# Scaling the tokens by their RMS factors before a plain transposition, in place of a product with a scaled identity

## The chip, the cores and the metric

The kernel runs on one core of a Trainium2 chip. The metric is the device time of one execution in microseconds (us), the median of several executions. A core has TensorE (PE in the profile, PEld its weight loads), VectorE (DVE), ScalarE (ACT), GpSimd (POOL) and SyncE (SP), each with a queue of instructions that it runs in order.

## The reference

Two layers of a diffusion backbone work on 512 latent tokens and 256 context tokens of width 1024. What matters here is the frame around the big products:

```python
def rms_norm(x, g):
    y = x * lax.rsqrt(jnp.mean(x * x, axis=-1, keepdims=True) + EPS)
    return y * g

for i in range(DEPTH):                      # DEPTH = 2
    h = modulate(rms_norm(x, norm_mix_pre[i]), sh1, sc1)
    m = mixing_sublayer(h, ...)             # ends with ... @ w_out[i], the out projection
    x = x + g1 * rms_norm(m, norm_mix_post[i])
    f = swiglu(modulate(rms_norm(x, norm_ffn_pre[i]), sh2, sc2), ...)
    x = x + g2 * rms_norm(f, norm_ffn_post[i])
```

In the second layer only the latent tokens go on to the output. All is in float32.

## The kernel before, in words

Tokens lie in six tiles of 128: tiles 0 and 1 are context, 2 to 5 latent. The second layer's out projection and FFN treat tiles 2 to 5 alone. The big products run on TensorE as three passes each (`mm3`, lines 142 to 144), because weights and activations are split in a high and a low part; `wblock` loads a block of weights (line 136, SP queue), ScalarE writes the high part (line 131) and VectorE the low one (line 132). Activations enter those products transposed, with the 1024 channels on the partitions: `hhi` and `hlo`.

At the end of an out projection (`out_proj`, lines 1089 to 1104) and of the first layer's FFN (`ffn`, lines 1190 to 1219) each token tile takes these steps:

1. ScalarE squares and sums the product (`square`, line 1026), VectorE multiplies it by the gate.
2. `residual`: GpSimd turns the sums into the factor of the post norm (`rsq`, lines 185, 187 and 188), VectorE adds the scaled product to the old tokens `xt` (line 1031).
3. GpSimd's queue issues the DMA of the new tokens to DRAM (line 1099 or 1212).
4. `norm_tile`: ScalarE sums the squares of the new tokens (line 330, two instructions), GpSimd makes the factor of the pre norm (lines 187 and 188), and ScalarE scales the 128x128 identity by it (line 337). The scaled identity `dg` lies in the first 128 columns of the tile's row in `ut` (out projection) or `mt` (FFN), where it shows in the profile as u or m.
5. After every second tile, `to_hT` transposes and scales the pair at once: for each of eight blocks of 128 channels, and for each of the two tiles, a matmul of 128x128 with the tokens as stationary operand and `dg` as moving one (line 147). Four of these fill one PSUM bank; the banks are the single ones of the pools pr and md in turn. ScalarE applies the modulation (line 351, two instructions for each bank), VectorE splits the result (lines 355 and 356).

There are 16 such tiles, in eight pairs: three pairs at the first out projection (profile 346 to 384 us), three at the end of the first FFN (946 to 986 us), two at the second out projection (1149 to 1183 us). The text calls these places site 1, 2 and 3. The same `to_hT` also serves the very start of the kernel with another call of `norm_tile`.

The order of instructions on each engine is set when the program is built: a planner simulates the engines with its own costs and gives each engine the next instruction that it holds to be ready, earlier lines of the program first. On the chip each engine then follows its list, whatever comes late.

Of the kernel before, what the change touches and what calls it, by code (L numbers as in the profile page):

```python
# [14 lines left out]
AF = mybir.ActivationFunctionType  # L15
ALU = mybir.AluOpType
# [68 lines left out]
def tile_backbone(ctx, tc, A, out):  # L85
# [60 lines left out]
    def mm(ps, lhsT, rhs, start=True, stop=True, **k):  # L146
        return PE.matmul(ps, lhsT, rhs, start=start, stop=stop, skip_group_check=True, **k)  # L147
# [185 lines left out]
    def norm_tile(x, dg, junk):  # L333

        ss = sumsq(x, junk)
        r = rsq(ss, 1, 1.0 / D)
        S.activation(dg, ident, AF.Copy, scale=r[:, 0:1])

    def to_hT(l, sub, pr, xs, dg, hhi, hlo, k2s=range(4), start=False):
        lane = 1 if pr == 0 else 0  # L340
        for k2 in k2s:
            ps = acc() if start else (mdt if k2 % 2 else prt)()
            for kk in range(2):
                for i in range(2):
                    k = 2 * k2 + kk
                    mm(ps[:, 256 * kk + 128 * i:256 * kk + 128 * i + 128],
                       xs[i][:, 128 * k:128 * k + 128], dg[i])
            h32 = sp.tile([128, 2, 256], F32, tag="h32", name=nm("h32"), bufs=2)
            for kk in range(2):
                k = 2 * k2 + kk  # L350
                last_s[0] = S.activation(h32[:, kk], ps[:, 256 * kk:256 * kk + 256], AF.Identity,
                                         scale=cols[l][:, 2 * sub, lane, k:k + 1],
                                         bias=cols[l][:, 2 * sub + 1, lane, k:k + 1])
            o = (slice(None), slice(2 * k2, 2 * k2 + 2), slice(256 * pr, 256 * pr + 256))
            V.tensor_copy(hhi[o], h32)
            last_v[0] = V.tensor_sub(hlo[o], h32, hhi[o])  # L356
# [680 lines left out]
    def out_proj(l, mac, Gs):  # L1037

        lat_only = l == DEPTH - 1
        tiles = list(range(2, 6)) if lat_only else list(range(6))  # L1040
        w_out = A["w_out"][l].rearrange("(k p) c -> p k c", p=128)
        src = [(mac, 0), (mac, 1), None, None, None, None, (mac, 2), (mac, 3)]
        order = (0, 6, 2, 4)

        def run(rnd, h, pss, ks=order):
            def one(i, k, w):
                o = slice(128 * i, 128 * i + 128)
                t_, c_ = src[k]
                mm3(pss[i], t_[:, 0, c_, o], t_[:, 1, c_, o], w[0][:, k % 2], w[1][:, k % 2],
                    k == order[0], k == order[-1] + 1)  # L1050

            last = {}
            for n, k in enumerate(ks):
                w = wblock(w_out[:, k:k + 2, 512 * h:512 * h + 512], [128, 2, 512])
                if ks[-1] == order[-1] and n >= len(ks) - 2 and h == 1:
                    last[k] = last[k + 1] = w
                    continue
                for kk in range(2):
                    for i in rnd:
                        one(i, k + kk, w)  # L1060
            for i in rnd:
                for k, w in last.items():
                    one(i, k, w)

        pss0 = {i: acc() for i in tiles[:3]}
        if lat_only:
            pss0[tiles[3]] = mdt()
        run(list(pss0), 0, pss0, order[:2])
        mb = yield
        for n in range(4):  # L1070
            src[2 + n] = (mb, n)
        late = [i for i in tiles if i not in pss0]
        for i in late:
            pss0[i] = aux()
        if late:
            run(late, 0, pss0, order[:2])
        h2 = [bigt([128, 8, 768], F32R, "h2") for _ in range(2)]
        ut = bigt([128, 6, 1024], F32, "u")
        sq = sums()
        half = 2 if lat_only else 3  # L1080
        xts, dg = {}, {}
        Gs = Gs()
        for rnd, h in ((tiles, 0), (tiles[:half], 1), (tiles[half:], 1)):
            pss = pss0 if h == 0 else {i: (acc if i in tiles[:min(half, 3)] else aux)() for i in rnd}
            if h == 1:
                for i in rnd:
                    xts[i] = q4([128, 1024], s="xt")
                    dma(xts[i], xd[i])
            run(rnd, h, pss, order if h else order[2:])
            for i in rnd:  # L1090
                square(pss[i], sq[i], h)
                c_ = slice(512 * h, 512 * h + 512)
                V.tensor_mul(ut[:, i, c_], pss[i], Gs[1 if i < 2 else 0][:, c_])
                if h == 0:
                    continue
                xt = xts[i]
                residual(xt, ut[:, i], sq[i])
                xo = dr.tile([128, 1024], F32, name=nm("xd"))
                dmap(xo, xt)
                xd[i] = xo  # L1100
                dg[i] = ut[:, i, 0:128]
                norm_tile(xt, dg[i], ut[:, i])
                if i % 2 == 1:
                    to_hT(l, 1, i // 2, (xts[i - 1], xts[i]), (dg[i - 1], dg[i]), *h2)
        yield h2

    def ffn(l, h2, filler):
# [5 lines left out]
        wg = A["ffn_w_gate"][l].rearrange("(k p) c -> p k c", p=128)  # L1113
        wu = A["ffn_w_up"][l].rearrange("(k p) c -> p k c", p=128)
        wd = A["ffn_w_down"][l].rearrange("(f p) c -> p f c", p=128)
        xts, dg = {}, {}
        act = [bigt([128, 8, 768], F32R, "act") for _ in range(2)]
        mt = bigt([128, 6, 1024], F32, "m")
        for pi, (f0, nf) in enumerate(parts):
# [61 lines left out]
            for rnd, h in rounds:  # L1181
# [11 lines left out]
                for i in rnd:  # L1193
# [6 lines left out]
                    if last and h == 1:  # L1200
                        xt = xts[i]
                        if lat_only:
                            r = rsq(sq[i][:, 0:1], 1, 1.0 / D, more=sq[i][:, 1:2])
                            for hf in range(2):
                                c_ = slice(512 * hf, 512 * hf + 512)
                                V.scalar_tensor_tensor(xt[:, c_], mt[:, i, c_], r[:, 0:1], xt[:, c_],
                                                       op0=ALU.mult, op1=ALU.add)
                                dma(out[0, 128 * (i - 2):128 * (i - 2) + 128, c_], xt[:, c_])
                            continue
                        residual(xt, mt[:, i], sq[i])  # L1210
                        xo = dr.tile([128, 1024], F32, name=nm("xd"))
                        dmap(xo, xt)
                        xd[i] = xo
                        dg[i] = mt[:, i, 0:128]
                        norm_tile(xt, dg[i], mt[:, i])
                        if i == 1:
                            hnext.extend(bigt([128, 8, 768], F32R, "h") for _ in range(2))
                        if i % 2 == 1:
                            to_hT(l + 1, 0, i // 2, (xts[i - 1], xts[i]), (dg[i - 1], dg[i]), *hnext)

    hnext = []

# [144 lines left out]
```

## Time and profile before

| what | value |
|---|---|
| median of three runs | 1559.03 us |
| the three runs | 1552.45, 1559.03, 2079.58 us |
| the profiled execution | 1553.79 us |
| its span, first to last instruction | 1552.0 us |
| mean granted TensorE clock in it | 0.987 of full |
| busy share of TensorE, VectorE, ScalarE, GpSimd | 95%, 54%, 41%, 10% |
| DMA, mean over the span | 162 GB/s |

The third run is a disturbed one. The profile lists for every instruction its start and its length. A matmul's length includes its way through the array, so a row of x8 matmuls that lasts 1.05 us with matmuls of 0.27 us each starts one every (1.05 - 0.27) / 7 = 0.11 us. The idle time in brackets behind a row is that of the engine just before it, with what ended it.

### The profile page before, as it was taken

What the parts mean: (1) busy time and instruction counts of PE and PEld (TensorE: products, weight loads), DVE (VectorE), ACT (ScalarE), POOL (GpSimd) and SP (SyncE); (2) the same over time, 40 slices, a digit from 0 to 9 for tenths busy, and PEclk for the clock granted to TensorE, in tenths of its full rate; (3) what the DMA queues carried; (4) which work ended last, traced back from release to release, by engine and by line L of the source; (5) the groups of instructions that cost most, each with busy time, mean ns of one, the idle gap of its engine ahead of it and who ended that gap; (6) DMA issues with size and microseconds to landing.
All of it is one profiled execution on the core that took longest, in us unless ns stands there. A gap on an engine that the chain in (4) does not pass through costs nothing.

```text
span 1552.0 us, 22603 instructions
## 1 busy us (share of the span) xinstructions
PE 1475.9 (95%) x8777; PEld 1227.6 (79%) x8777; DVE 841.0 (54%) x1479; ACT 630.7 (41%) x1182; POOL 161.1 (10%) x281
## 2 busy tenths in 40 slices
PE   4899898999999999999999999999988999999996
PEld 3766695888888778888778887899778888888885
DVE  5977864646465676445763336587555332333334
ACT  3778564446323234233222215656454223222222
POOL 1113210012000010000010005211011000000003
PEclk9999999999999999999999999999999999999998
DMA  9788987773334455333674314768474333333332
GB/s 294 246 274 262 306 273 220 254 181 108 92 109 121 138 185 175 111 95 118 209 261 128 95 62 130 235 170 240 112 265 135 95 95 97 99 102 97 96 95 82
DMA packets 219487, 250.68 MB, mean 162 GB/s; under 512 B 41806, under 2 KB 164058, under 8 KB 218868
## 3 DMA queue, kind: packets, MB, share of 16 engines
q1 hardware_dynamic: 209268, 214.26, 45.5%
q0 software_dynamic: 9344, 34.58, 6.4%
q8 instruction: 69, 1.13, 0.3%
q10 hardware_dynamic: 768, 0.40, 0.1%
q14 instruction: 38, 0.31, 0.1%
HBM read 206.76 MB, written 42.43 MB: 161 GB/s over the span
## 4 chain that ended last, share of the span: by engine, by line
PE 81%; DMA 9%; DVE 4%; ACT 3%; POOL 1%; issue 1%; SPq 1%; DVEq 0%; POOLq 0%; ACTq 0%
PE acc L142 20%; PE acc L144 19%; PE acc L143 19%; PE aux L144 4%; PE aux L142 4%; PE aux L143 4%; PE pr L147 3%; PE md L147 3%; PE aux L147 2%; DMA F<-Fd 2%; DMA raw<-in_w_out_dram 1%; DMA wm<-in_w_mod_dram 1%; DVE w L132 1%; DMA raw<-in_w_in_dram 1%; PE acc L147 1%
## 5 line engine op out<-in xcount | busy, mean ns | idle before, releaser
L142 PE MATMUL acc<-h,w 128*128 128x512 f32 (+1 forms) x1248 | 430.1, 346 | 1.2 <-ACT w L131 0.8
L144 PE MATMUL acc<-h,w 128*128 128x512 f32 (+1 forms) x1248 | 428.4, 344 | 2.8 <-DVE w L132 2.8
L143 PE MATMUL acc<-h,w 128*128 128x512 f32 (+1 forms) x1248 | 429.5, 345 | 1.5 <-DVE h L356 1.4
L132 DVE TENSOR_TENSOR w<-raw,w 128x1024 fp32r<-128x1024 f32 x190 | 233.0, 1227 | 335.1 <-ACT w L131 332.3
L131 ACT CAST w<-raw 128x1024 fp32r<-128x1024 f32 x190 | 199.3, 1050 | 411.7 <-PE acc L143 231.3
L142 PEld LDWEIGHTS acc<-h,w 128*128 128x128 f32 x1248 | 235.8, 190 | 33.6 <-issue 3.4
L144 PEld LDWEIGHTS acc<-h,w 128*128 128x128 f32 x1248 | 236.1, 189 | 33.1 <-DVE w L132 3.6
L143 PEld LDWEIGHTS acc<-h,w 128*128 128x128 f32 x1248 | 236.3, 189 | 30.8 <-DVE h L356 2.3
L1142 DVE TENSOR_TENSOR fsg<-fsg,acc 128x512 f32<-128x512 f32 (+1 forms) x68 | 39.8, 585 | 159.7 <-PE acc L144 156.8
L144 PE MATMUL aux<-w,act 128*128 128x512 f32 x220 | 86.2, 393 | 0.0
L143 PE MATMUL aux<-w,act 128*128 128x512 f32 x220 | 86.2, 392 | 0.0
L144 PE MATMUL acc<-w,act 128*128 128x512 f32 x220 | 86.0, 391 | 0.0
L143 PE MATMUL acc<-w,act 128*128 128x512 f32 x220 | 85.8, 390 | 0.0
L142 PE MATMUL aux<-w,act 128*128 128x512 f32 x220 | 82.7, 390 | 0.0
L142 PE MATMUL acc<-w,act 128*128 128x512 f32 x220 | 82.5, 392 | 0.0
L266 DVE SCALAR_TENSOR_TENSOR macc<-wm,csil,macc 128x1024 f32<-128x1024 f32 x56 | 70.6, 1278 | 5.5 <-DMA wm<-in_w_mod_dram 5.4
L1143 ACT CAST act<-fsg 128x512 fp32r<-128x512 f32 (+1 forms) x68 | 36.5, 537 | 87.5 <-DVE fsg L1142 87.5
L1141 ACT ACTIVATE fsg<-acc 128x512 f32<-128x512 f32 (+1 forms) x68 | 34.8, 511 | 81.4 <-PE acc L144 81.4
L143 PE MATMUL acc<-w,h 128*128 128x512 f32 (+1 forms) x160 | 55.6, 348 | 1.1 <-DVE w L132 1.1
L147 PE MATMUL md<-wm,csil 128*32 128x256 f32 (+1 forms) x416 | 35.6, 404 | 21.1 <-DMA wm<-in_w_mod_dram 21.1
L144 PE MATMUL acc<-w,h 128*128 128x512 f32 (+1 forms) x160 | 55.2, 345 | 0.0
L142 PE MATMUL acc<-w,h 128*128 128x512 f32 (+1 forms) x160 | 53.9, 354 | 0.0
(370 smaller groups left out, 2322.8 us busy)
## 6 DMA issues: line engine op xcount, KB each, us to landing
wm<-in_w_mod_dram SPq DMA_DIRECT2D x90, 512.0 KB, 4.3
raw<-in_ffn_w_gate_dram SPq DMA_DIRECT2D x44, 512.0 KB, 3.9
raw<-in_ffn_w_up_dram SPq DMA_DIRECT2D x44, 512.0 KB, 3.8
raw<-in_ffn_w_down_dram SPq DMA_DIRECT2D x44, 512.0 KB, 3.8
raw<-in_w_in_dram SPq DMA_DIRECT2D x28, 512.0 KB, 5.0
raw<-in_w_out_dram SPq DMA_DIRECT2D x26, 512.0 KB, 6.9
xt<-xd SPq DMA_DIRECT2D x18, 512.0 KB, 4.9
Ed<-Et POOLq DMA_DIRECT2D x16, 512.0 KB, 4.7
```

Source lines behind the costliest of these rows:

```text
L131: S.copy(hi, raw)
L132: last_v[0] = V.tensor_sub(lo, raw, hi)
L142: PE.matmul(ps, lhi, rhi, start=start, stop=False, skip_group_check=True)
L143: PE.matmul(ps, lhi, rlo, start=False, stop=False, skip_group_check=True)
L144: return PE.matmul(ps, llo, rhi, start=False, stop=stop, skip_group_check=True)
L147: return PE.matmul(ps, lhsT, rhs, start=start, stop=stop, skip_group_check=True, **k)
L266: V.scalar_tensor_tensor(accs[r], raw, c_, accs[r], op0=ALU.mult, op1=ALU.add)
L1141: S.activation(sg[:, :n], p1[:, :n], AF.Silu)
L1142: V.tensor_mul(sg[:, :n], sg[:, :n], p2[:, :n])
L1143: S.copy(act[0][:, fl, o:o + n], sg[:, :n])
```

## The change

A new helper writes the scaled tokens themselves: ScalarE the first 512 channels, GpSimd the other 512, both into the tile's row of `ut` or `mt`. `to_hT` then gets these rows and no `dg`, and transposes them with the unscaled identity. The start of the kernel keeps the old way.

```diff
+    def norm_scaled(x, dst):
+
+        r = rsq(sumsq(x, dst), 1, 1.0 / D)
+        S.activation(dst[:, 0:512], x[:, 0:512], AF.Copy, scale=r[:, 0:1])
+        GP.tensor_scalar(dst[:, 512:1024], x[:, 512:1024], r[:, 0:1], None, op0=ALU.mult)
+
     def to_hT(l, sub, pr, xs, dg, hhi, hlo, k2s=range(4), start=False):
...
-                    mm(ps[:, 256 * kk + 128 * i:256 * kk + 128 * i + 128],
-                       xs[i][:, 128 * k:128 * k + 128], dg[i])
+                    o = ps[:, 256 * kk + 128 * i:256 * kk + 128 * i + 128]
+                    x_ = xs[i][:, 128 * k:128 * k + 128]
+                    PE.transpose(o, x_, ident) if dg is None else mm(o, x_, dg[i])
...
-                dg[i] = ut[:, i, 0:128]
-                norm_tile(xt, dg[i], ut[:, i])
+                norm_scaled(xt, ut[:, i])
                 if i % 2 == 1:
-                    to_hT(l, 1, i // 2, (xts[i - 1], xts[i]), (dg[i - 1], dg[i]), *h2)
+                    to_hT(l, 1, i // 2, (ut[:, i - 1], ut[:, i]), None, *h2)
...
-                        dg[i] = mt[:, i, 0:128]
-                        norm_tile(xt, dg[i], mt[:, i])
+                        norm_scaled(xt, mt[:, i])
...
-                            to_hT(l + 1, 0, i // 2, (xts[i - 1], xts[i]), (dg[i - 1], dg[i]), *hnext)
+                            to_hT(l + 1, 0, i // 2, (mt[:, i - 1], mt[:, i]), None, *hnext)
```

## Rows read from the trace of the kernel before

**Rows 1.** The page, part 1: busy us, share of the span, instructions of each engine.

```profile
PE 1475.9 (95%) x8777; PEld 1227.6 (79%) x8777; DVE 841.0 (54%) x1479; ACT 630.7 (41%) x1182; POOL 161.1 (10%) x281
```

**Rows 2.** Groups of TensorE by line and shape: busy us, mean ns | idle before.

```profile
L147 PE MATMUL pr<-u,xt 128*128 128x128 f32 x80 | 13.7, 310 | 5.2 <-ACT u L337 3.9 <-ACT h L351 1.3
...
L147 PE MATMUL md<-u,xt 128*128 128x128 f32 x80 | 12.4, 292 | 1.5 <-ACT h L351 1.5
...
L147 PE MATMUL pr<-m,xt 128*128 128x128 f32 x48 | 7.1, 280 | 1.1 <-ACT h L351 1.1
L147 PE MATMUL md<-m,xt 128*128 128x128 f32 x48 | 7.0, 279 | 0.4 <-ACT h L351 0.4
...
L533 PE MATMUL pr<-ident,Cr 128*128 128x128 f32 x16 | 2.9, 313 | 0.0
```

**Rows 3.** Timeline of TensorE at and behind site 1: start us, us, instruction, count.

```profile
357.16 1.05 PE L147 MATMUL pr<-u,xt 128*128 128x128 f32 x8
...
363.28 1.65 PE L147 MATMUL pr<-u,xt 128*128 128x128 f32 x6 [0.83 <-ACT u L337]
...
378.04 0.83 PE L147 MATMUL pr<-u,xt 128*128 128x128 f32 x6
...
412.73 0.60 PE L533 MATMUL pr<-ident,Cr 128*128 128x128 f32 x4
```

**Rows 4.** Timeline of ScalarE at site 1.

```profile
364.97 1.02 ACT L351 ACTIVATE h<-pr,cols 128x256 f32<-128x256 f32 x2 [1.74 <-PE pr L147]
...
374.33 0.40 ACT L337 ACTIVATE u<-ident,rs 128x128 f32<-128x128 f32 x1 [0.96 <-POOL rs L188]
```

**Rows 5.** Stretches: length, busy of PE, PEld, DVE, ACT, POOL, clock, DMA.

```profile
360.00:365.00 5.00, 2.69 (x12) 2.31 (x13) 4.21 (x6) 2.35 (x6) 2.44 (x5) 0.79 0.62 210
370.00:380.00 10.00, 10.00 (x54) 8.58 (x53) 2.80 (x5) 5.00 (x10) 2.23 (x4) 1.00 0.13 52
946.00:961.00 15.00, 15.00 (x70) 12.49 (x69) 10.82 (x15) 8.19 (x18) 6.77 (x16) 1.00 0.19 74
961.00:980.00 19.00, 15.62 (x116) 13.79 (x115) 15.14 (x23) 15.04 (x33) 10.71 (x21) 1.00 0.89 286
```

**Rows 6.** Two lines of GpSimd: ns of one, shortest/median/longest, first and last start.

```profile
L798 POOL COPY wk<-PT x16: 498/1027/5005, 77.6 to 1067.6; 128x384 f32<-128x384 f32 x16
...
L1198 POOL TENSOR_TENSOR m<-m,G x10: 1282/1300/2272, 936.2 to 1527.8; 128x512 f32<-128x512 f32 x10
```

**Rows 7.** Groups of ScalarE by line and shape: busy us, mean ns.

```profile
L1143 ACT CAST act<-fsg 128x512 fp32r<-128x512 f32 x42 | 26.1, 621 | 84.4 <-DVE fsg L1142 84.4
...
L337 ACT ACTIVATE u<-ident,rs 128x128 f32<-128x128 f32 x10 | 4.0, 402 | 8.1 <-POOL rs L188 8.1
```

**Rows 8.** Timeline of GpSimd at site 2, tile 3 to tile 4.

```profile
967.28 0.33 POOL L187 TENSOR_SCALAR rs<-ss 128x1 f32<-128x1 f32 x1 [0.68 <-ACT m L330]
...
968.83 0.39 POOL L187 TENSOR_SCALAR rs<-rs 128x1 f32<-128x1 f32 x1
969.30 0.55 POOL L188 TENSOR_TENSOR rs<-rs,mhalf 128x1 f32<-128x1 f32 x1
```

**Rows 9.** Timeline of VectorE at site 2.

```profile
938.51 1.79 DVE L132 TENSOR_TENSOR w<-raw,w 128x1024 fp32r<-128x1024 f32 x1
...
969.88 1.28 DVE L1031 SCALAR_TENSOR_TENSOR xt<-m,rs,xt 128x1024 f32<-128x1024 f32 x1 [0.72 <-POOL rs L188]
```

**Rows 10.** Timelines of ScalarE and TensorE at the last tile of site 2.

```profile
979.05 0.40 ACT L337 ACTIVATE m<-ident,rs 128x128 f32<-128x128 f32 x1 [0.19 <-POOL rs L188]
...
979.50 0.94 PE L147 MATMUL pr<-m,xt 128*128 128x128 f32 x6
```

**Rows 11.** Timelines of GpSimd and TensorE at site 3.

```profile
1169.22 1.78 POOL L187 TENSOR_SCALAR rs<-ss 128x1 f32<-128x1 f32 x1 [0.36 <-ACT u L330]
...
1169.13 0.39 PE L144 MATMUL acc<-h,w 128*128 128x256 f32 x1 [1.79 <-DVE w L132]
...
1177.24 0.94 PE L147 MATMUL pr<-u,xt 128*128 128x128 f32 x6 [2.11 <-ACT u L337]
```

More of the change, by code (lines that the diff above doesn't have):

```diff
@@ L1080, in out_proj @@
         half = 2 if lat_only else 3
-        xts, dg = {}, {}
+        xts = {}
         Gs = Gs()
@@ L1115, in ffn @@
         wd = A["ffn_w_down"][l].rearrange("(f p) c -> p f c", p=128)
-        xts, dg = {}, {}
+        xts = {}
         act = [bigt([128, 8, 768], F32R, "act") for _ in range(2)]
```

## Prediction, made before the changed kernel was built

> **What bounds the kernel now.** I read the page's busy shares first: TensorE is busy for 95% of the span [rows 1], so time goes where its work goes, except where it waits. Next came the groups of TensorE, to see what the edited matmuls cost and what they wait for. They show 80 + 80 + 48 + 48 = 256 instructions for 16 tiles of 8 channel blocks, so each float32 matmul is two passes; and their waits are 5.2 + 1.5 + 1.1 + 0.4 = 8.2 us, half of that on the scaled identity [rows 2]. Then the timelines and stretches of the three sites, to see whether TensorE or the chain from tile to tile sets the pace. At site 1 TensorE waits for the second pair (2.69 us busy of 5 at a mean granted clock of 0.79) and is full through the third (10.00 of 10) [rows 5]. At site 2 it is full up to 961 us and busy for 15.62 of the next 19 us, while VectorE and ScalarE are busy for 15 each [rows 5]. There the pace is that of a chain: VectorE's residual is released by GpSimd 0.72 us after it was free [rows 9], and GpSimd had made that factor directly behind the factor of the tile before [rows 8]. The last tile's matmuls start 0.05 us after its identity is ready [rows 10]. At site 3 the last pair is waited for, 2.11 us [rows 11].
>
> **TensorE's part.** Eight half passes last 1.05 us: one starts every 0.11 us [rows 3]. Plain transpositions of the same shape are in the trace: line 533 transposes 2 x 2 x 4 = 16 blocks, and has 16 instructions [rows 2], four of them in 0.60 us, again 0.11 us apart [rows 3]. So a transposition costs half of a scaling matmul. A pair goes from 32 instructions to 16 and saves 16 x 0.111 = 1.78 us of TensorE; eight pairs save 14.2 us. That is the most that the edit can give.
>
> **ScalarE's part.** 16 scalings of the identity, 0.40 us each, give way to 16 of 128x512. The same engine's cast of 128x512 is 0.62 us [rows 7]; I take 0.60, so +0.2 us in each tile's chain. The squares, the sums and the factor stay.
>
> **GpSimd's part.** 16 new instructions on 128x512, price p. Below: a copy of 128x384 took 0.50 us at its shortest [rows 6], by columns 0.50 x 512 / 384 = 0.67 us, and a little less if a part of it is fixed. Above: the product of two 128x512 tiles, 1.28 us alone and 2.27 at its longest [rows 6]. Nearest is the copy, one input as here; I take p = 0.65 and keep 0.5 to 2.27 for the range. The Trainium skill (GPSIMD Engine Reference, 3.1, Elementwise) gives a measured 769 ns for 512 elements in a tight one-input loop; with that figure the sum below would be 0.7 us higher.
>
> TensorE needs this half only from the third bank of a pair on, and the banks pr and md come free at ScalarE's pace (1.02 us for each bank, [rows 4]); so for the pair itself p is hidden up to about 2 us (0.6 for ScalarE's half, 0.4 for the first bank's four transpositions, 1.0 until that bank is free). What is queued behind it on GpSimd matters more. The planner takes earlier lines of the program first, so the new instruction should stand behind the factor of tile i and ahead of the last step of the factor for tile i+1, for which VectorE's residual waits. Where one tile's factor directly follows another's, as in [rows 8], each handover costs p. There are four at site 1, five at site 2, two at site 3. GpSimd's queue also issues the DMA of the new tokens, now p later; they are read back behind it on the SP queue, but the next weights on that queue are more than 10 us away, so I cost that at nothing. If that cover were gone, it would be p once per tile. Tokens come free earlier, since TensorE no longer reads them: nothing, as no wait names them.
>
> **The sum by sites.**
> - Site 1: of the first pair's halves one (0.9 us) is among products without waits; the other ends in a wait for ScalarE and counts nothing. The second pair is exposed: ScalarE waited 1.74 us for its first bank [rows 4], behind six half passes at the low clock (1.65 us, [rows 3], against 0.83 for the same six at full clock); three transpositions would come 0.7 us sooner, less 0.2 for ScalarE: -0.5. The third pair: -1.78, TensorE being full there [rows 5]; its last tile's identity is ready at 374.7 us [rows 4] and used at 378.0 [rows 3], so the two handovers ahead of it are covered by 3.3 us. Sum -3.2 us.
> - Site 2: the first two pairs' relief (3.6 us) is lost in the wait for tile 5, for [rows 10] show no slack. Handovers 5 x p, less about 0.5 us of slack at the early tiles, where TensorE is full [rows 5]; +0.2 for ScalarE. The last pair -1.6. Sum 5p - 1.9 = +1.35 us.
> - Site 3: the first pair's relief falls in a wait for weights (1.79 us on line 132, [rows 11]): nothing, and its handover likewise. Handover from tile 4 to 5: p + 0.2. The last pair ran at a lowered clock; paced by ScalarE, I take -1.0. Sum p - 0.8 = -0.15 us.
>
> Together 6p - 5.9 = -2.0 us at p = 0.65. Against the profiled execution's 1553.79 us (span 1552.0 and 1.8 around it) this gives **1552 us**. The median shown is 5.2 us above that execution, with only three runs, one disturbed; a new median may stand as far off, which the range takes in.
>
> **Rivals.**
> - **GpSimd becomes the slower link** (slower than before). p decides at 1.0 us: above it 6p - 5.9 is a loss. For it: VectorE and GpSimd hold each other up here. A factor step of 128x1, 0.19 us elsewhere, took 1.78 us while VectorE split tokens [rows 11], the product of line 1198 went from 1.28 to 2.27 [rows 6], and VectorE's split beside it took 1.79 [rows 9]. At p = 2.27 the sum is +7.7, and two handovers (4.5 us) outrun the 3.3 us of slack at site 1, +1.2: 1553.8 + 8.9 = 1562.7 us. Against it: the planner may put the scaling where GpSimd waits for the residual, 1.3 us each time. The Trainium skill (SBUF — State Buffer, Who interferes with whom) says that a VectorE instruction with two SBUF inputs and a GpSimd instruction that reads SBUF exclude each other for the whole instruction, whoever comes first. The rows named here agree with it; by that rule taken alone every handover would cost the long price. Chance 0.2.
> - **TensorE's relief counts in full**: the planner fills the gaps with other products, and the scaling stands off the chain. 1553.8 - 14.2 = 1539.6 us. For it: the 95% of [rows 1]. Against it: the waits at all three sites [rows 2]. Chance 0.15.
> - **The planner's list changes far from the sites**, with weights and products in another order; either sign, of unknown size, and the one way to more than 2%. Chance 0.06.
> - **A plain transposition is no cheaper** (two passes after all): nothing gained, 6p + 0.6 lost, 1558 us. [Rows 2] speak against it, 16 calls and 16 instructions. Chance 0.02.
>
> **Numbers.** The forecast, 1545 to 1558 us by its own bounds (p from 0.5 to 1.3, a pair more or less), has 0.57. The range 1540 to 1564 reaches to the full relief and to the long price. 2% is 31 us, about what a measurement of this kernel can tell from no change; no case worked out comes near it, only a re-planned program could: faster 0.02, same 0.95, slower 0.03.
>
> **What the changed profile would show.** 128 transpositions at sites 1 to 3 in place of 256 half passes, 0.11 us apart; ScalarE scalings near 0.60 us; a GpSimd row of 16 with a median near 0.65 us. At site 2, residuals of successive tiles further apart than the 5.3 to 5.5 us from tile 3 to 5, about p each, and more TensorE idle time between 961 and 980 us than the 3.4 us of before; at site 1 less TensorE work and no new wait. If the GpSimd row's median is over 1 us, the first rival is on; if the scaling stands behind the next tile's factor, my handovers are wrong; if TensorE's waits on these lines stay near 8 us while 14 us of work are gone, the second rival is.

## The result, and the profile after

The changed kernel is slower: **1566.09 us** median of 14 runs (1561.18 to 1575.05) against 1554.43 us of 14 runs of the kernel before. The ratio is 1.010, 95% interval 1.0076 to 1.0125, which is 12 to 19 us. It is taken from the undisturbed runs themselves (all but the one of 2079.58 us), not from the two medians, which would give 1.0075, 11.7 us. The median is above the range (1540 to 1564) and on the other side of the forecast's sign. The loss is less than 2%. The profiled execution after is 1563.76 us, its span 1561.6.

Page, part 1, against [rows 1]: TensorE has 128 instructions fewer and is busy for 5.4 us less, GpSimd has 16 instructions and 34.5 busy us more; the span is 9.6 us longer.

```profile
PE 1470.5 (94%) x8649; PEld 1220.2 (78%) x8649; DVE 841.6 (54%) x1479; ACT 635.7 (41%) x1182; POOL 195.6 (13%) x297
```

The two new lines. GpSimd's line 343 by shape: ns of one, shortest/median/longest, first and last start:

```profile
L343 POOL TENSOR_SCALAR u<-xt,rs x10: 1568/1575/2505, 338.9 to 1185.8; 128x512 f32<-128x512 f32 x10
L343 POOL TENSOR_SCALAR m<-xt,rs x6: 1567/1572/1752, 951.4 to 986.5; 128x512 f32<-128x512 f32 x6
```

ScalarE's line 342 in the groups (busy us, mean ns):

```profile
L342 ACT ACTIVATE u<-xt,rs 128x512 f32<-128x512 f32 x10 | 7.2, 724 | 5.3 <-POOL rs L188 5.3
```

GpSimd's scaling takes 1.57 us where I took 0.65, ScalarE's 0.72 where I took 0.60. The transpositions and their waits, against [rows 2] (line 147 became line 354):

```profile
L354 PE MATMUL pr<-ident,u 128*128 128x128 f32 x40 | 8.8, 332 | 14.0 <-ACT u L342 8.0 <-ACT h L358 3.1 <-POOL rs L188 1.7
L354 PE MATMUL md<-ident,u 128*128 128x128 f32 x40 | 8.6, 328 | 0.8 <-ACT h L358 0.8
...
L354 PE MATMUL pr<-ident,m 128*128 128x128 f32 x24 | 6.1, 373 | 7.8 <-ACT m L342 5.4 <-POOL rs L188 1.9 <-issue 0.5
L354 PE MATMUL md<-ident,m 128*128 128x128 f32 x24 | 5.3, 336 | 0.2 <-ACT h L358 0.2
```

The waits went from 8.2 us to 14.0 + 0.8 + 7.8 + 0.2 = 22.8 us. They name ScalarE's line 342 first, and ScalarE's line waits for the factor of GpSimd. What holds the factor back is seen in the timeline of GpSimd at site 2, tile 3 to tile 4, the place of [rows 8]:

```profile
972.40 0.56 POOL L188 TENSOR_TENSOR rs<-rs,mhalf 128x1 f32<-128x1 f32 x1
973.05 0.20 POOL L187 TENSOR_SCALAR rs<-rs 128x1 f32<-128x1 f32 x1
973.34 1.57 POOL L343 TENSOR_SCALAR m<-xt,rs 128x512 f32<-128x512 f32 x1
974.88 0.56 POOL L188 TENSOR_TENSOR rs<-rs,mhalf 128x1 f32<-128x1 f32 x1
```

In [rows 8] line 187 is followed by line 188 at once. Now the scaling of tile 3 stands between these two steps of tile 4's factor, for which VectorE's residual waits. The chain of waits through this stretch has the scaling as a link (pieces: start us, us, what):

```profile
964.03 1.25 POOL rs L187
965.56 0.71 POOL rs L188
966.35 0.65 POOL rs L187
967.10 1.75 POOL m L343
968.85 0.55 POOL rs L188
969.42 1.30 DVE xt L1038
970.74 1.16 ACT m L330 x2
...
986.43 0.73 ACT m L342
987.21 0.90 PE pr L354 x3
```

The six residuals of site 2 (xt by m; first and last start after x6), before and after, one fence for each kernel:

```profile
L1031 DVE SCALAR_TENSOR_TENSOR xt<-m,rs,xt x6: 1283/1284/1285, 949.7 to 975.2; 128x1024 f32<-128x1024 f32 x6
```

```profile
L1038 DVE SCALAR_TENSOR_TENSOR xt<-m,rs,xt x6: 1271/1284/1286, 947.2 to 983.0; 128x1024 f32<-128x1024 f32 x6
```

They span 25.5 us before and 35.8 after; I call this the residual spread. Two more sites answer to [rows 3, 4, 11]. TensorE's waits for the second pair of site 1, the last of site 2 and the last of site 3:

```profile
361.38 0.90 PE L354 MATMUL pr<-ident,u 128*128 128x128 f32 x3 [4.53 <-ACT u L342]
...
987.21 0.90 PE L354 MATMUL pr<-ident,m 128*128 128x128 f32 x3 [4.16 <-ACT m L342]
...
1187.15 0.90 PE L354 MATMUL pr<-ident,u 128*128 128x128 f32 x3 [3.45 <-ACT u L342]
```

And the stretches of [rows 5], with one more behind them (columns as there):

```profile
360.00:365.00 5.00, 3.10 (x14) 2.56 (x15) 1.92 (x4) 3.25 (x6) 3.20 (x6) 0.50 0.12 48
370.00:380.00 10.00, 9.40 (x49) 7.56 (x48) 2.80 (x4) 5.94 (x10) 3.23 (x5) 1.00 0.13 52
946.00:961.00 15.00, 13.82 (x68) 11.30 (x66) 11.15 (x15) 9.62 (x20) 9.64 (x17) 1.00 0.32 111
961.00:980.00 19.00, 12.62 (x58) 10.71 (x59) 11.37 (x19) 12.06 (x26) 11.53 (x18) 0.69 0.85 272
980.00:1000.00 20.00, 15.32 (x80) 13.30 (x79) 8.87 (x13) 8.77 (x16) 5.76 (x7) 0.78 0.41 143
```

From 961 to 980 us TensorE is idle for 6.4 us where it was idle for 3.4, and the granted clock is 0.69 where it was 1.00; at site 1 it is at the lower of its two levels, 1.2 GHz, through the whole of 360 to 365 us. At site 1 it falls at 357.3 us, after TensorE had stood still for 3.12 and 0.58 us and 0.5 us into the wait of 4.53; the first fall at site 2, at 964.9 us, comes behind waits of 1.37, 0.24, 0.44 and 1.15 us between 960 and 965 us.

To set the sites apart I measured stretches between starts of ScalarE's casts of weight blocks (line 131, line 133 in e2_gp_later; 190 of them in each kernel): from the 28th to the 33rd is site 1, from the 94th to the 103rd site 2, from the 120th to the 131st site 3. They are of one execution each, read to about 0.1 us, and so good for differences of several us only.

The 103rd cast is a mark that moves. In after and in the kernels e1, e2, e4, e6 and e12 of the experiments below the planner puts it earlier: VectorE starts 4 instructions between the 102nd and the 103rd there, and 17 or 18 in the other nine kernels. From the 104th on to the 120th, the second layer's mixing, the lists of ScalarE, VectorE and GpSimd are the same in all fifteen. So the stretch from the 94th to the 104th is the one to compare between all kernels; the one to the 103rd is kept because the expectations name it.

Each ratio is to runs of the kernel before made beside that kernel (their medians lie between 1549.95 and 1554.43 us), so the medians of two kernels are not to be compared directly.

| kernel | site 1 | site 2 | site 2, to the 104th | mixing 2, from the 104th | site 3 | residual spread, site 2 | ratio to before (95%) |
|---|---|---|---|---|---|---|---|
| before | 48.3 | 75.2 | 82.8 | 133.2 | 62.5 | 25.5 | 1 |
| after | 50.8 | 84.1 | 96.4 | 131.4 | 62.7 | 35.8 | 1.010 (1.0076 to 1.0125) |
| e3_dead_gp | 52.0 | 85.6 | 95.2 | 128.8 | 61.4 | 35.2 | 1.0115 (1.0084 to 1.0145) |
| e5_dve_half | 48.6 | 75.4 | 82.9 | 131.8 | 60.1 | 26.2 | 0.9991 (0.9974 to 1.0009) |
| e1_act_all | 48.9 | 74.1 | 85.3 | 132.0 | 63.1 | 26.7 | 1.003 (1.001 to 1.0049) |
| e4_gp_128 | 48.1 | 79.2 | 91.6 | 132.0 | 62.5 | 30.3 | 1.0059 (1.0037 to 1.008) |
| e6_gp_tt | 48.4 | 79.8 | 90.9 | 132.3 | 61.9 | 31.6 | 1.0077 (1.0046 to 1.0108) |
| e9_gp_pipe | 50.8 | 76.7 | 83.8 | 131.9 | 62.8 | 26.1 | 1.0005 (0.9987 to 1.0023) |
| e2_gp_later | 49.1 | 80.4 | 92.8 | 134.5 | 62.9 | 31.4 | 1.0107 (1.0086 to 1.0128) |
| e12_gp_site2 | 48.3 | 84.1 | 96.6 | 130.6 | 61.8 | 35.2 | 1.0058 (1.0038 to 1.0077) |
| e13_gp_site13 | 50.1 | 75.2 | 82.8 | 131.4 | 62.3 | 26.2 | 1.0019 (1.0004 to 1.0033) |
| e8_dve_mm | 48.9 | 77.5 | 84.9 | 132.7 | 61.3 | 26.2 | 1.0002 (0.9981 to 1.0024) |
| e7_dve_pipe | 52.8 | 73.3 | 81.6 | 131.9 | 60.2 | 21.1 | 1.0017 (0.9995 to 1.0039) |
| e10_dve_pipe23 | 48.3 | 73.0 | 81.5 | 135.2 | 59.3 | 21.0 | 0.9978 (0.9952 to 1.0004) |
| e11_before_pipe23 | 48.5 | 75.4 | 83.5 | 134.4 | 59.8 | 22.3 | 1.0012 (0.9993 to 1.003) |

Between the sites nothing moves: the 33rd to the 94th cast takes 540.1 us in all fifteen, the 131st to the end 345.3 or 345.4. Ahead of the 28th, where nothing was changed, single executions take 335.0 to 346.2 us; the one of after is 4.9 us shorter there than the one of before. From the 28th to the 131st after is 14.5 us longer, where the spans differ by 9.6: 13.6 of it at site 2, 2.5 at site 1, 0.2 at site 3 and -1.8 in the mixing.

### The profile page after: what moved, and what is told of

Same layout as the page of the kernel before. It is cut to its first block, busy times and chain, and to the rows that moved or that the text cites. A ratio compares the mean times of both kernels' runs of the same rounds, so it can differ in the third digit from the quotient of the medians.

```text
span 1561.6 us, 22365 instructions
## 1 busy us (share of the span) xinstructions
PE 1470.5 (94%) x8649; PEld 1220.2 (78%) x8649; DVE 841.6 (54%) x1479; ACT 635.7 (41%) x1182; POOL 195.6 (13%) x297
## 4 chain that ended last, share of the span: by engine, by line
PE 78%; DMA 6%; DVE 6%; ACT 4%; POOL 2%; issue 2%; SPq 1%; DVEq 0%; POOLq 0%; ACTq 0%
PE acc L142 19%; PE acc L144 19%; PE acc L143 19%; PE aux L144 4%; PE aux L142 4%; PE aux L143 4%; PE pr L147 2%; PE aux L147 2%; PE md L147 2%; DMA wm<-in_w_mod_dram 1%; DVE w L132 1%; DMA yd<-zslot 1%; ACT w L131 1%; DMA E<-Ed 1%; DVE xt L1038 1%
## 5 line engine op out<-in xcount | busy, mean ns | idle before, releaser
L142 PE MATMUL acc<-h,w 128*128 128x512 f32 (+1 forms) x1248 | 435.6, 351 | 3.5 <-ACT w L131 1.6
L143 PE MATMUL acc<-h,w 128*128 128x512 f32 (+1 forms) x1248 | 434.3, 349 | 3.8 <-DVE h L363 3.7
L144 PE MATMUL acc<-h,w 128*128 128x512 f32 (+1 forms) x1248 | 432.1, 347 | 0.8 <-DVE w L132 0.8
L142 PEld LDWEIGHTS acc<-h,w 128*128 128x128 f32 x1248 | 240.2, 193 | 37.2 <-issue 3.4
L143 PEld LDWEIGHTS acc<-h,w 128*128 128x128 f32 x1248 | 240.8, 193 | 33.8 <-DVE h L363 4.8
L144 PEld LDWEIGHTS acc<-h,w 128*128 128x128 f32 x1248 | 240.4, 193 | 30.4 <-issue 1.5
L1204 POOL TENSOR_TENSOR m<-m,G 128x512 f32<-128x512 f32 x10 | 14.8, 1508 | 360.4 <-ACT jk L1033 360.4
```

The costliest lines, as they stand in the source:

```text
L142: PE.matmul(ps, lhi, rhi, start=start, stop=False, skip_group_check=True)
L143: PE.matmul(ps, lhi, rlo, start=False, stop=False, skip_group_check=True)
L144: return PE.matmul(ps, llo, rhi, start=False, stop=stop, skip_group_check=True)
L1204: (GP if h == 0 else V).tensor_tensor(mt[:, i, c_], mt[:, i, c_], Gs[1 if i < 2 else 0][:, c_], op=ALU.mult)
```

## The experiments

### Is it GpSimd's instruction?

My theory after the comparison: GpSimd's 16 instructions, queued ahead of the next tile's factor, are the loss. That is Q, the queue, in the expectations. Its rivals are on TensorE's side (T: the transposition waits for two scaled halves in place of a small identity) and on ScalarE's (S: the longer scaling there is the loss). Three kernels tell them apart.

**e3_dead_gp**: the kernel before, and behind each `norm_tile` of the three sites GpSimd's new instruction, into columns that nobody reads. Scaled identity and two-pass product stay.

```diff
         S.activation(dg, ident, AF.Copy, scale=r[:, 0:1])
+        if dead:
+            GP.tensor_scalar(junk[:, 512:1024], x[:, 512:1024], r[:, 0:1], None, op0=ALU.mult)
```

> The kernel before with the scaled identity and its matmuls, plus the new GpSimd instruction (128x512, 1.57 us in the changed kernel) at the same place, its result read by nobody. Theory Q (the instruction stands in GpSimd's list between the steps of the next tile's factor and lengthens the chain from residual to residual): slower than before by at least as much as the change, ratio 1.010 to 1.020, as nothing of TensorE's relief is there; the six residuals of site 2 spread over about 35 us as in the changed kernel, against 25.5 before. Rival T (half as many TensorE passes leave TensorE idle at the sites, its clock falls and the rest follows): ratio 1.00, clock at site 2 as before. Rival S (the longer ScalarE scaling, 0.72 against 0.40 us): ratio 1.00.

Measured 1564.61 us, ratio 1.0115 (1.0084 to 1.0145): the whole loss, with nobody waiting for the result and with all of TensorE's and ScalarE's old work. The granted clock falls here too (0.86 from 961 to 980 us, 0.79 from 980 to 1000), so it does not take the halved passes of T to lower it. The instruction lasts as long as in the changed kernel:

```profile
L339 POOL TENSOR_SCALAR u<-xt,rs x10: 1568/1574/2502, 341.0 to 1184.5; 128x512 f32<-128x512 f32 x10
L339 POOL TENSOR_SCALAR m<-xt,rs x6: 1567/1575/2022, 954.9 to 989.5; 128x512 f32<-128x512 f32 x6
```

**e5_dve_half**: the change, with the second half on VectorE.

```diff
-        GP.tensor_scalar(dst[:, 512:1024], x[:, 512:1024], r[:, 0:1], None, op0=ALU.mult)
+        V.tensor_scalar(dst[:, 512:1024], x[:, 512:1024], r[:, 0:1], None, op0=ALU.mult)
```

> The changed kernel with the second half of the columns scaled on VectorE in place of GpSimd. Theory Q: residuals of site 2 back to about 26 us, VectorE's instruction about 0.4 us, ratio 0.993 to 1.000. Rival T: ratio 1.008 or more and a lowered clock. Rival S: about 1.005, ScalarE's 0.72 us being there still.

Measured 1549.35 us, ratio 0.9991 (0.9974 to 1.0009); the residual spread is back at 26.2 us. VectorE needs 0.49 us for the half that takes GpSimd 1.57:

```profile
L343 DVE TENSOR_SCALAR u<-xt,rs x10: 485/486/491, 346.3 to 1176.7; 128x512 f32<-128x512 f32 x10
```

So the loss goes with GpSimd's instruction, and what is left of the change gains nothing that can be told from zero.

**e1_act_all**: all 1024 channels on ScalarE, no GpSimd.

```diff
-        S.activation(dst[:, 0:512], x[:, 0:512], AF.Copy, scale=r[:, 0:1])
-        GP.tensor_scalar(dst[:, 512:1024], x[:, 512:1024], r[:, 0:1], None, op0=ALU.mult)
+        S.activation(dst, x, AF.Copy, scale=r[:, 0:1])
```

> The changed kernel with all 1024 columns scaled on ScalarE, nothing new on GpSimd. Theory Q: residuals of site 2 back to about 26 us, ratio 0.995 to 1.000, ScalarE's instruction about 1.2 us. Rival T: the transpositions are still half of the passes, so the clock at sites 1 and 2 stays low and the ratio stays at 1.008 or more. Rival S: worse than the change, 1.012 or more, as each tile waits 0.5 us longer for ScalarE.

Measured 1556.28 us, ratio 1.003 (1.001 to 1.0049), above what I expected (0.995 to 1.000). ScalarE's instruction is 1.15 us, 0.43 longer than the half: on the path (site 2 to the 104th cast is 85.3 us, 2.4 more than with VectorE's half), and dearer than I thought, but a fraction of GpSimd's loss.

### Its length or its place?

**e4_gp_128**: GpSimd scales 128 columns, ScalarE 896.

```diff
-        S.activation(dst[:, 0:512], x[:, 0:512], AF.Copy, scale=r[:, 0:1])
-        GP.tensor_scalar(dst[:, 512:1024], x[:, 512:1024], r[:, 0:1], None, op0=ALU.mult)
+        S.activation(dst[:, 0:896], x[:, 0:896], AF.Copy, scale=r[:, 0:1])
+        GP.tensor_scalar(dst[:, 896:1024], x[:, 896:1024], r[:, 0:1], None, op0=ALU.mult)
```

> The changed kernel with GpSimd scaling the last 128 columns alone and ScalarE the other 896. Theory Q with a price by columns: 0.19 + 1.38 x 128 / 512 = 0.53 us for GpSimd's instruction, ScalarE's about 1.04; residuals of site 2 over about 29 us, ratio 1.004 to 1.007, between ScalarE alone (1.003) and the change (1.010). Rival K (it is the presence of a GpSimd instruction there, blocked by or blocking VectorE, not its length): ratio about 1.010.

Measured 1561.71 us, ratio 1.0059 (1.0037 to 1.008), spread 30.3 us: as expected. A quarter of the columns still costs 0.61 us at the median (mean 0.76 at site 2, 0.94 at the others), ScalarE's part 1.05.

```profile
L343 POOL TENSOR_SCALAR m<-xt,rs x6: 605/614/1316, 950.4 to 980.1; 128x128 f32<-128x128 f32 x6
```

**e6_gp_tt**: the same half on GpSimd as a product of two inputs, the factor spread over the columns.

```diff
-        GP.tensor_scalar(dst[:, 512:1024], x[:, 512:1024], r[:, 0:1], None, op0=ALU.mult)
+        GP.tensor_tensor(dst[:, 512:1024], x[:, 512:1024], bc(r[:, 0:1], [128, 512]), op=ALU.mult)
```

> The changed kernel with GpSimd's 16 instructions as products of two inputs (the factor spread over 512 columns) in place of an operation with one factor for each partition. If the length of GpSimd's instruction sets the loss, and a two-input product is 1.28 us as at line 1198 where the present one is 1.57: about 0.3 us less for each handover, residual gaps of 6.6 to 7 us at site 2 in place of 7.2, ratio 1.006 to 1.009. If it is the place in GpSimd's list whatever the length: ratio 1.008 to 1.012, the same as the change. If it is slower than 1.57: 1.011 to 1.015.

Measured 1561.39 us, ratio 1.0077 (1.0046 to 1.0108), spread 31.6 us. The instruction is shorter than expected, 1.04 us, and the spread fell by 4.2 us. The ratio lies where the first expectation put it, but its interval holds the second one too; it is the spread that speaks for the length.

```profile
L343 POOL TENSOR_TENSOR m<-xt,rs x6: 1040/1042/1495, 954.5 to 985.4; 128x512 f32<-128x512 f32 x6
```

In the order of GpSimd's median, none, 0.61, 1.04 and 1.57 us, the spread is 26.2, 30.3, 31.6 and 35.8 us and the ratio 0.9991, 1.0059, 1.0077 and 1.010. (The second also has 0.33 us more on ScalarE.) From none to 1.57 us the spread grows by 9.6 us, 1.92 for each of five handovers; for 0.61 and 1.04 us it is 0.82 and 1.08 for each.

**e9_gp_pipe**: the changed kernel with GpSimd's 16 instructions as they are, but a tile's squares, factor, scaling and transposition written behind the next tile's residual, at all three sites (shown for site 1).

```diff
-                norm_scaled(xt, ut[:, i])
-                if i % 2 == 1:
-                    to_hT(l, 1, i // 2, (ut[:, i - 1], ut[:, i]), None, *h2)
+                todo.append(i)
+                if len(todo) > 1:
+                    finish(todo.pop(0))
+            while todo:
+                finish(todo.pop(0))
```

`finish(j)` holds the three removed lines for tile j.

> The changed kernel (GpSimd's half of 1.57 us) with each tile's pre norm and transposition written behind the residual of the next tile. Theory Q: most handovers are gone, as the next factor is issued ahead of the scaling; residuals of site 2 over about 25 us, ratio 0.996 to 1.004. Rival: the GpSimd instruction costs by its sheer length wherever it stands: ratio 1.008 to 1.012.

Measured 1552.65 us, ratio 1.0005 (0.9987 to 1.0023), spread 26.1 us. The loss is gone, though each instruction is longer than in the changed kernel (mean 1.83 and 1.97 us against 1.72 and 1.61):

```profile
L343 POOL TENSOR_SCALAR u<-xt,rs 128x512 f32<-128x512 f32 x10 | 18.3, 1834 | 1.0
...
L343 POOL TENSOR_SCALAR m<-xt,rs 128x512 f32<-128x512 f32 x6 | 11.8, 1969 | 0.4
```

Against the same order with VectorE's half (e7_dve_pipe, 1.0017, below) they cost nothing that can be told from zero (-0.0012, 0.0028 either way); in the order of the changed kernel they cost 0.0109 (0.0030 either way, against e5_dve_half). So it is the place that makes them dear.

Length counts through the place: the scaling costs as much as it lengthens the way from one residual to the next. It is not off that way altogether in this order either. GpSimd and VectorE, same kernel:

```profile
972.32 2.42 POOL L343 TENSOR_SCALAR m<-xt,rs 128x512 f32<-128x512 f32 x1
974.82 0.19 POOL L187 TENSOR_SCALAR rs<-rs 128x1 f32<-128x1 f32 x1
975.07 0.64 POOL L1227 DMA_DIRECT2D xd<-xt  x1
975.74 0.59 POOL L188 TENSOR_TENSOR rs<-rs,mhalf 128x1 f32<-128x1 f32 x1
```

```profile
976.36 1.28 DVE L1038 SCALAR_TENSOR_TENSOR xt<-m,rs,xt 128x1024 f32<-128x1024 f32 x1 [2.98 <-POOL rs L188]
```

The residual still waits behind a scaling there. But the other work between two residuals became shorter: with VectorE's half this order has a spread of 21.1 us (e7_dve_pipe, below), and GpSimd's instructions bring it up to 26.1, about what it was before.

**e2_gp_later**: in the changed kernel the even tiles' GpSimd half is held until the next tile's post-norm factor has been issued.

```diff
+    def release():
+        while held:
+            x, dst, r = held.pop()
+            with tc.issue_after(last_r[0].ins):
+                GP.tensor_scalar(dst[:, 512:1024], x[:, 512:1024], r[:, 0:1], None, op0=ALU.mult)
```

> The changed kernel, but the GpSimd half of every even tile is held back until the factor of the next tile's residual has been issued; the same 16 instructions of the same length. Theory Q: three of five handovers at site 2 and one or two at each other site lose their 1.57 us, residuals of site 2 over about 31 us, ratio 1.003 to 1.006. Rivals T and S: as the change, 1.010, since TensorE's and ScalarE's work is the same.

Measured 1566.46 us, ratio 1.0107 (1.0086 to 1.0128): a miss. The spread fell to 31.4 us as expected, and sites 1 and 2 (to the 104th cast) are 5.3 us shorter than after, but the time did not follow; in the one profiled execution the second layer's mixing is 3.1 us longer than after, on the same lists. By its time this kernel leaves the place undecided; e9_gp_pipe decided it.

### At which site?

**e12_gp_site2** and **e13_gp_site13**: the helper gets its engine; GpSimd at site 2 and VectorE elsewhere, and the other way round.

```diff
-                norm_scaled(xt, ut[:, i])
+                norm_scaled(xt, ut[:, i], V)
...
-                        norm_scaled(xt, mt[:, i])
+                        norm_scaled(xt, mt[:, i], GP)
```

> GpSimd scales the second half at site 2 alone (6 instructions), VectorE at sites 1 and 3. If the loss lies where the stretches put it, at site 2's five handovers: ratio 1.005 to 1.008, residual spread of site 2 about 35 us, site 2 about 84 us. If every handover counts alike wherever it is (site 2 has 5 of 12): 1.003 to 1.005. If the loss lies at sites 1 and 3: 0.998 to 1.002.

> The other way round: GpSimd's half at sites 1 and 3 (10 instructions), VectorE's at site 2. If the loss lies at site 2: ratio 1.000 to 1.003, site 2 as with VectorE's half (75 us, spread 26 us). If every handover counts alike: 1.005 to 1.007. If the two kernels' losses together stay far below the 1.0 per cent of the change, the sites act on one another, through the list that the planner makes or through the clock.

Measured 1561.4 us, ratio 1.0058 (1.0038 to 1.0077), for GpSimd at site 2, and 1554.51 us, 1.0019 (1.0004 to 1.0033), for GpSimd at sites 1 and 3. Against e5_dve_half the six instructions of site 2 cost 0.0067 (10.4 us, 4.1 either way when the two half widths are joined as squares) and the ten others 0.0028 (4.3 us, 3.5 either way). With e5_dve_half's -0.0009 the parts sum to 1.0086, inside the interval of the change. So site 2 carries most of it, as its stretch said (84.1 us in after and e12_gp_site2, 75.2 in e13_gp_site13; to the 104th cast 96.4 and 96.6 against 82.8).

### What is TensorE's relief worth?

**e8_dve_mm**: e5_dve_half with the two-pass product back, against the unscaled identity; TensorE has its old 256 passes.

```diff
-                    PE.transpose(o, x_, ident) if dg is None else mm(o, x_, dg[i])
+                    mm(o, x_, ident if dg is None else dg[i])
```

> The variant with VectorE's half, but transposed by a matmul with the unscaled identity (two passes) in place of the plain transposition: TensorE has its 14.2 us of passes back, all else is the same. Theory W (at the sites TensorE waits for the chain from tile to tile, so its relief is lost in waits and in a lower clock): ratio 0.998 to 1.003, as without (0.9991). Rival: the relief counts, and its loss costs most of 14 us: ratio 1.006 to 1.008.

Measured 1551.52 us, ratio 1.0002 (0.9981 to 1.0024), where the same kernel with plain transpositions has 0.9991. The difference is 0.0011, 1.7 us, with 4.3 either way (the two ran on different chips, each beside runs of the kernel before): 14.2 us in full is excluded, zero is not. Stretches of the kernel with transpositions and then of the one with products:

```profile
961.00:980.00 19.00, 14.21 (x75) 11.43 (x73) 15.44 (x23) 15.33 (x30) 10.71 (x21) 0.82 0.89 298
980.00:1000.00 20.00, 18.88 (x103) 16.10 (x104) 12.58 (x20) 11.25 (x20) 1.75 (x3) 0.91 0.61 202
```

```profile
961.00:980.00 19.00, 14.49 (x101) 12.54 (x99) 15.60 (x23) 15.56 (x30) 10.98 (x20) 1.00 0.87 253
980.00:1000.00 20.00, 18.79 (x116) 16.08 (x116) 10.34 (x18) 10.53 (x20) 1.31 (x3) 1.00 0.63 223
```

With 39 instructions fewer TensorE is busy as long, 33.09 against 33.28 us, at a clock of 0.82 and 0.91 in place of 1.00. Over the whole execution the mean granted clock of the 12 runs is 0.9795 against 0.985. That VectorE and ScalarE, busy for 15 of the 19 us in both, set the pace is my reading of these rows.

### A better order

**e7_dve_pipe**: the order of e9_gp_pipe with VectorE's half.

> The variant with VectorE's half, with each tile's pre norm and transposition written behind the residual of the next tile, so that the planner takes the next residual's factor first. Theory W: the chain from residual to residual is cut, the six residuals of site 2 lie over about 20 us (25.5 before), ratio 0.990 to 0.997. Rival (the sites are bound by the work of TensorE, ScalarE and VectorE, not by the chain): 0.998 to 1.001.

Measured 1553.64 us, ratio 1.0017 (0.9995 to 1.0039), a miss. The spread fell by 5 us to 21.1, site 2 by 2.1; site 1 is 4.2 us longer than in e5_dve_half. There the pair's transposition comes one tile later; that TensorE had no other work to fill that time with is my reading and was not isolated.

**e10_dve_pipe23**: the same at sites 2 and 3 alone, in the first layer's out projection as in e5_dve_half.

```diff
+                todo.append(i)
+                if len(todo) > lat_only:
+                    finish(todo.pop(0))
```

`lat_only` is 0 at site 1 and 1 at site 3.

> The version with VectorE's half (e5_dve_half), with a tile's norm and transposition written behind the next tile's residual at site 2 and site 3 alone; site 1 as in e5_dve_half. By the stretches of the runs with and without this order (site 1: 48.6 against 52.8 us; site 2: 75.4 against 73.3; site 3: 60.1 and 60.2) the order is worth 2 us at site 2, nothing more at site 3, and costs 4 us at site 1. If these add up: about 1548 to 1550 us, ratio 0.995 to 0.999, a residual spread of site 2 near 21 us, site 1 near 48.6. If the stretches don't add up because the list is planned anew and the work behind the sites shifts: 0.999 to 1.003.

Measured 1547.65 us, ratio 0.9978 (0.9952 to 1.0004), site 1 at 48.3 us and the spread at 21.0 us as expected. It beats the changed kernel, and its ratio is the lowest of all, but its interval reaches past 1, so it is not shown to beat the kernel before.

**e11_before_pipe23**: the kernel before in that order, scaled identity and two passes kept.

> The kernel before (scaled identity, two-pass product) with the same order at sites 2 and 3. If at site 2 the chain from tile to tile sets the pace, and not TensorE, its residual spread falls from 25.5 to about 21 us as in e7_dve_pipe and the time with it by 2 us or so: ratio 0.996 to 1.000. If the saving belongs to the cheaper transposition, the spread falls and the stretch of site 2 (75.2 us) does not: 0.999 to 1.002.

Measured 1551.62 us, ratio 1.0012 (0.9993 to 1.003). The spread fell to 22.3 us and site 2's stretch did not (75.4 against 75.2; to the 104th cast 83.5 against 82.8). My reading, not isolated, is that with the two-pass product TensorE has that time to fill anyway. The cheaper transposition and the shorter chain seem to need each other, but 0.9978 against 1.0012 is a difference of 0.0034 with 0.0032 either way, just told from zero.

## Why the prediction was wrong

**The price of GpSimd's instruction** is the step that failed: "Nearest is the copy, one input as here; I take p = 0.65". It was 1.57. The kind of operation decided, not the number of inputs: an operation with a factor for each partition took 1.57 us for 512 columns and 0.61 for 128, 2.5 ns for each column ((1.57 - 0.61) / 384) and 0.29 fixed; the copy of [rows 6] took 0.50 us for 384 columns. The other row that I had, 1.28 us for the two-input product, was nearer. The figure of the Trainium skill (GPSIMD Engine Reference, 3.1, Elementwise) that I gave, 769 ns for 512 elements in a tight loop, is not given there for this operation, which took twice as long; the measurement decides. I had said that break-even is at p = 1.0, so the sign of the forecast hung on this one number.

**Where the instruction stands** was right for site 2: ahead of the last step of the next factor, one price for each of five handovers. That gave 5 x 1.57 - 0.5 = 7.4 us at the real price; e12_gp_site2 measured 10.4 (6.3 to 14.5), and the spread grew by 1.92 for each handover. Against the kernel before it grew by 10.3 us, and the timelines of the one execution after account for most of that: 8.1 us are the five scalings (1.57 to 1.75 us each), and 1.8 us are two residuals that found VectorE taken when their factor was ready. The first of these is the residual of tile 2. Its factor was ready at 960.26 us (GpSimd's line 188, 959.61 + 0.65):

```profile
958.17 1.65 DVE L132 TENSOR_TENSOR w<-raw,w 128x1024 fp32r<-128x1024 f32 x1 [0.26 <-ACT w L131]
...
960.35 1.21 DVE L132 TENSOR_TENSOR w<-raw,w 128x1024 fp32r<-128x1024 f32 x1
961.48 1.27 DVE L1038 SCALAR_TENSOR_TENSOR xt<-m,rs,xt 128x1024 f32<-128x1024 f32 x1
```

A split of weights that did not wait for the factor had gone ahead of the residual. The prediction has no term for this.

**Site 1 was wrong** in "no new wait" and in its handovers: four were named, but in the sum for the site stand only the two ahead of the third pair, as covered. Those two did stay covered: from tile 3 to 5 the DMAs of the new tokens are as far apart as before (6.52 and 7.22 us against 6.48 and 7.08), and TensorE is busy for 9.40 of the 10 us from 370 to 380. But the handovers from tile 0 to 1 and 1 to 2, put at nothing without a reason, cost 2.47 us each (7.88 and 6.96 us from DMA to DMA against 5.41 and 4.49). Before, GpSimd had stood idle ahead of tile 3's factor:

```profile
356.06 0.22 POOL L185 TENSOR_TENSOR rs<-ss 128x1 f32<-128x1 f32 x1 [3.86 <-ACT jk L1026]
```

The two costs used up these 3.86 us, and so the scaling stands in the way from tile 2 to 3 too, at 2.00 us, a handover that the count left out:

```profile
352.38 0.25 POOL L185 TENSOR_TENSOR rs<-ss 128x1 f32<-128x1 f32 x1
352.61 2.00 POOL L343 TENSOR_SCALAR u<-xt,rs 128x512 f32<-128x512 f32 x1
354.70 0.19 POOL L187 TENSOR_SCALAR rs<-rs 128x1 f32<-128x1 f32 x1
354.97 1.56 POOL L188 TENSOR_TENSOR rs<-rs,mhalf 128x1 f32<-128x1 f32 x1
```

TensorE's wait for the second pair went from 0.83 us [rows 3] to 4.53, at the lower clock. Sites 1 and 3 together cost 4.3 us (0.8 to 7.8) with GpSimd, where one handover, 1.6 us, was in the sum.

**TensorE's relief was still too high.** Without GpSimd's terms the sum has -5.4 us (-5.9 less the 0.5 of slack for the handovers); without GpSimd the change measured -1.4 (-4.0 to +1.4), though VectorE's 0.49 us for each tile is in that. I gave site 1's third pair in full (-1.78), because TensorE was full there [rows 5], and site 2's last pair nearly so (-1.6) without a reason. But with fewer passes TensorE was busy as long at a lower granted clock (e8_dve_mm); as I read those rows, the pair goes at the pace of ScalarE and VectorE. **ScalarE** was 0.12 us a tile too cheap (0.72, taken 0.60).

**The sum again.** With p = 1.57 the formula gives 6 x 1.57 - 5.9 = +3.5 us. The parts as measured are 10.4 (site 2) + 4.3 (sites 1 and 3) - 1.4 (the rest) = 13.3 us, against 12 to 19 measured for the change. So a right price alone would have turned the sign, and it is 5.5 of the 15.3 us between -2.0 and +13.3; the relief is 4.0, site 2's surplus over its five prices 3.0, the handovers at sites 1 and 3 2.7. All but the price carry the widths given above.

**The rivals.** "GpSimd becomes the slower link" came true, through p above its point of decision, as the prediction said a median over 1 us would show. But its reason, that VectorE and GpSimd hold each other up, is a small part in GpSimd's scalings: 13 of 16 instructions lasted 1.57 to 1.63 us, the others 1.75, 2.00 and 2.50. The longest began as VectorE's split did:

```profile
1163.60 2.50 POOL L343 TENSOR_SCALAR u<-xt,rs 128x512 f32<-128x512 f32 x1
```

```profile
1163.43 1.23 DVE L132 TENSOR_TENSOR w<-raw,w 128x1024 fp32r<-128x1024 f32 x1 [1.05 <-ACT w L131]
```

That one case is as the Trainium skill has it (SBUF — State Buffer, Who interferes with whom): a two-input VectorE instruction and a GpSimd instruction that reads SBUF exclude each other, and the scaling, second to come, ended 1.44 us after the split did, about its own length. At none of site 2's five handovers was the long price of 2.27 us paid. Two products of two SBUF inputs began early in a scaling there, and it was VectorE's instruction that took longer: the split at 958.17 us shown above, 1.65 us where the median is 1.23, and this one, 1.06 where it is 0.69.

```profile
980.81 1.63 POOL L343 TENSOR_SCALAR m<-xt,rs 128x512 f32<-128x512 f32 x1
```

```profile
981.03 1.06 DVE L363 TENSOR_TENSOR h<-h,h 128x512 fp32r<-128x512 f32 x1
```

It ended 0.35 us before the scaling did, so here, as far as GpSimd's spans can be read that closely, neither was held off for the other's whole instruction; the measurement decides. "TensorE's relief counts in full" is excluded by e8_dve_mm. "A plain transposition is no cheaper" is refuted by the trace: 128 instructions, and four of them in 0.60 us at full clock, 0.11 apart:

```profile
351.89 0.60 PE L354 MATMUL md<-ident,u 128*128 128x128 f32 x4
```

"The planner's list changes far from the sites" is not what happened: the stretches between the sites are alike, and the lists of ScalarE, VectorE and GpSimd from the 104th cast to the 120th are the same in all kernels. What changed is the place of the 103rd cast, at the end of site 2.

**Left open.** The second layer's mixing, from the 104th cast on, takes 128.8 to 135.2 us in the one profiled execution of each kernel, on the same lists of these three engines; why is not known, and it limits what the stretches can tell. What the earlier 103rd cast costs by itself is not isolated; e3_dead_gp has the longer site 2 (95.2 us to the 104th cast) without it, so the loss does not need it. The size of TensorE's relief is known only as 1.7 us with 4.3 either way.

## What to carry to other kernels

Before an instruction is put on an engine with a short list, ask what stands behind it there: here 16 instructions of 1.57 us on an engine busy for 13% cost more than 14 us of TensorE passes were worth, because at site 2 and at the first tiles of site 1 they stood between two steps that the next tile waited for. Price an instruction by a row of the same operation on the same engine; where there is none, work out at which price the sign turns and let the chance of the other sign be as large as the doubt about it. Work taken from an engine that waits in turn with others came back here as waits and a lower granted clock, so count only what the slowest link of that stretch gets rid of.

## What the hardware showed that was not expected

- On GpSimd an operation with one factor for each partition (1.57 us for 128x512) is slower than a product of two inputs with that factor spread over the columns (1.04), and three times slower than on VectorE (0.49).
- ScalarE's scaled copy took 0.72 us for 512 columns, 1.05 for 896 and 1.15 for 1024.
- With fewer TensorE passes in a stretch that waits on other engines, the granted clock was lower (0.82 and 0.91 against 1.00 in 961 to 1000 us; 0.9795 against 0.985 over all runs), with the same busy time.
- A VectorE product of two SBUF inputs that began 0.22 us into a GpSimd scaling of 1.63 us took 1.06 us in place of 0.69 and ended first; a GpSimd scaling that began 0.17 us into such a product took 2.50 in place of 1.57.
